# An encoder trunk in split fp32: h and the S forms at other SBUF addresses, S sums issued in the gate chunk

## The chip, the cores and the metric

The kernel runs on one core of a Trainium2 chip. The metric is the device time of one execution in microseconds (us).

## The reference

Two layers of a streaming encoder on 256 tokens with a model width of 2048, in float32. What matters here is the second half of each layer, the feed-forward part with an inner width of 5632:

```python
for l in range(DEPTH):
    ...                                   # attention, retention, w_out
    x = layer_norm(ALPHA * x + mix, ln1_g[l], ln1_b[l])
    f = (jax.nn.silu(x @ w_gate[l]) * (x @ w_up[l])) @ w_down[l]
    x = layer_norm(ALPHA * x + f, ln2_g[l], ln2_b[l])
return x
```

## The kernel before

**Split operands.** Each float32 operand is split into a high and a low part in a faster 4-byte format (ScalarE copies the high part, VectorE subtracts it for the low one, `split`, lines 249 to 251). A product is three matmuls: high by high, high weights' low part, low by high (lines 238 to 240, and 795 to 797). The activations are stationary, 128 by 128; the split weights are streamed, 512 columns. Weights come as units of 512 rows by 512 columns: a DMA on SP's queue brings a raw tile, the split fills one of three pairs of buffers `hi` and `lo` (lines 165 to 193), `W.get` hands the unit to the matmuls, and `W.done` prepares the unit that is three further on. One unit is 24 matmuls for both token halves.

**The feed-forward part.** The inner width is cut into 11 blocks of 512. Block 0 is the plain group (lines 769 to 783): a gate chunk of four units into the banks `gb`, SiLU on ScalarE, then the S forms, then an up chunk of four units into `ub`. Blocks 1 to 10 are Strassen groups (lines 785 to 861): for the first 1024 rows of `w_gate` and `w_up` the gate and the up product are joined by Strassen's scheme (the two token halves and the two weights form the 2 by 2 blocks), the other 1024 rows are multiplied plainly; together 15 products of 12 matmuls, in the banks sX, sQ, sW, sY, sZ and sR. Their stationary operands are slices of x (`xTh`, `xTl`) and the four S forms (`sfh`, `sfl`), sums of quarters of x that are computed once per layer: four subtractions on VectorE, 16 transposes on TensorE into banks `pts`, four splits (lines 744 to 755). A group's result is transposed into `hTh` and `hTl` by `flush`, eight transposes in banks `pth`, which the next group or the down-projection calls (lines 759 to 767). The blocks are taken in four parts of 3, 3, 2 and 3 blocks; behind each part comes its down-projection (lines 875 to 886) into banks `db`, with h stationary and the weights streamed, for four quarters of the output columns.

**Order.** The first three gate units are run for token half 0 and then for half 1 (`chunk_head`, lines 300 to 315), with the last pieces of the layer norm popped in between; these write the residual tile `res`, from which the S sums read. On each engine the instructions run in the order in which the program holds them.

**Addresses.** Tiles stand in SBUF in the order in which their pools first ask for them. In the program before, `hi` and `lo` stand at 192 modulo 256 bytes per partition, `xTh` and `xTl` at 128, `sfh` and `sfl` at 128, then a pad of 384 bytes (line 863), then `hTh` and `hTl` at 0, the vectors `v` at 0, and the raw tiles of the Strassen groups at 0.

Of the kernel before, what the change touches and what calls it, by code (L numbers as in the profile page):

```python
# [10 lines left out]
F32 = mybir.dt.float32  # L11
# [7 lines left out]
P = 128  # L19
# [92 lines left out]
def trunk(ctx: ExitStack, tc: tile.TileContext, x, pos, w, lnp, cols, eye, consts, out):  # L112
    nc = tc.nc
    V, A, PE, G = nc.vector, nc.scalar, nc.tensor, nc.gpsimd
# [8 lines left out]
    xTh = const.tile([P, KD, S], F32R, name="xTh")  # L123
    xTl = const.tile([P, KD, S], F32R, name="xTl")
# [7 lines left out]
    ident = const.tile([P, P], F32, name="ident")  # L132
    const.tile([P, 88], F32, name="pad0")

    def bank(tag_name):
        return psp.tile([P, 512], F32, tag="ps", name=tag_name)
# [96 lines left out]
    def mm_x(ps, ncol, tok, unit, xh, xl, k0, nk, first, last):  # L233
        wh, wl = unit
        for k in range(nk):
            sh = xh[:, k0 + k, tok * P:(tok + 1) * P]
            sl = xl[:, k0 + k, tok * P:(tok + 1) * P]
            PE.matmul(ps[:, :ncol], sh, wh[:, k, :ncol], start=first and k == 0, stop=False)  # L238
            PE.matmul(ps[:, :ncol], sh, wl[:, k, :ncol], start=False, stop=False)  # L239
            PE.matmul(ps[:, :ncol], sl, wh[:, k, :ncol], start=False, stop=last and k == nk - 1)  # L240
# [8 lines left out]
    def split(hi, lo, src):  # L249
        A.copy(hi, src)  # L250
        V.tensor_tensor(lo, src, hi.bitcast(F32), ALU.subtract)  # L251
# [36 lines left out]
    def pop(n=1):  # L288
        for _ in range(n):
            if pend:  # L290
                pend.pop(0)()

    def chunk_plain(banks, ncol, nu, xh, xl, k0, first=True, last=True):
        for u in range(nu):
            (unit,) = W.get()
            for tok in range(2):
                mm_x(banks[tok], ncol, tok, unit, xh, xl, k0 + 4 * u, 4, first and u == 0, last and u == nu - 1)
            W.done()

    def chunk_head(banks, ncol, nu, xh, xl):  # L300
        units = W.get(3)
        for u in range(3):
            mm_x(banks[0], ncol, 0, units[u], xh, xl, 4 * u, 4, u == 0, False)
            pop(1)
        pop(1)
        for u in range(3):
            mm_x(banks[1], ncol, 1, units[u], xh, xl, 4 * u, 4, u == 0, False)
            W.done()
            pop(1)
        pop(8)  # L310
        for u in range(3, nu):
            (unit,) = W.get()
            for tok in range(2):
                mm_x(banks[tok], ncol, tok, unit, xh, xl, 4 * u, 4, False, u == nu - 1)
            W.done()
# [55 lines left out]
    first = W.start()  # L371
# [45 lines left out]
    for l in range(DEPTH):  # L417
# [9 lines left out]

        cq = [bank(f"cq{t}") for t in range(2)]
        chunk_head(cq, 512, 4, xTh, xTl)
        if l == 0:  # L430
            rope_tables()
        ckv = [bank(f"ckv{t}") for t in range(2)]
        chunk_plain(ckv, 320, 4, xTh, xTl, 0)

        cqTh = att.tile([P, 4, S], F32R, tag="s1", name="cqTh")
# [117 lines left out]
        for t in range(2):  # L553
            pt = bank("pqr")
# [162 lines left out]
        mixh, mixl = Mix(mixAh, mixRh), Mix(mixAl, mixRl)  # L717
        wb = [bank(f"wo2{t}") for t in range(2)]
        chunk_plain(wb, 512, 4, mixh, mixl, 0)
        for t in range(2):  # L720
            resid(wb, 2, t, norm)
# [13 lines left out]
        ffp = ff_ctx.enter_context(tc.tile_pool(name=f"ff{l}", bufs=1))  # L735
        W.rpool = ff_ctx.enter_context(tc.tile_pool(name=f"rs{l}", bufs=3))
        normf = Norm(f"f{l}")
        sfh = ffp.tile([P, 4, 4, P], F32R, tag="sfh", name="sfh")
        sfl = ffp.tile([P, 4, 4, P], F32R, tag="sfl", name="sfl")

        def vt512(name):
            return ffp.tile([P, 512], F32, tag="v", bufs=8, name=name)

        def s_forms():
            x_ = lambda t, c: res[:, t, 512 * c:512 * (c + 1)]
            s1, s2, s3, s4 = (vt512(f"sf{i}") for i in range(4))
            V.tensor_tensor(s1, x_(1, 0), x_(1, 1), ALU.subtract)
            V.tensor_tensor(s2, x_(0, 0), s1, ALU.subtract)
            V.tensor_tensor(s3, x_(1, 0), x_(0, 0), ALU.subtract)
            V.tensor_tensor(s4, x_(0, 1), s2, ALU.subtract)  # L750
            for i, t in enumerate((s1, s2, s3, s4)):
                pt = bank("pts")
                for j in range(4):
                    PE.transpose(pt[:, j * P:(j + 1) * P], t[:, j * P:(j + 1) * P], ident)
                split(sfh[:, i, :, :], sfl[:, i, :, :], pt.rearrange("p (j t) -> p j t", j=4))

        hprev = []
# [10 lines left out]

        def plain_group(c, flush):
            gb = [bank(f"gb{t}") for t in range(2)]  # L770
            chunk_head(gb, 512, 4, xTh, xTl)
            sg = []
            for t in range(2):
                s_ = vt512("sg")
                A.activation(s_, gb[t], AF.Silu)
                sg.append(s_)
            flush()
            s_forms()
            ub = [bank(f"ub{t}") for t in range(2)]
            chunk_plain(ub, 512, 4, xTh, xTl, 0)  # L780
            for t in range(2):
                V.tensor_tensor(sg[t], sg[t], ub[t], ALU.mult)
                hprev.append((t, c, sg[t]))
# [76 lines left out]
            hprev.append((0, c, v2))  # L860
            hprev.append((1, c, v5))

        ffp.tile([P, 96], F32, tag="pad", name="pad1")
        for f0, f1 in FF_PARTS:
            nk = 4 * (f1 - f0)
            hTh = ffp.tile([P, 12, S], F32R, tag="hTh", name="hTh")
# [2 lines left out]
            for c in range(f0, f1):  # L869
                (strassen_group if c else plain_group)(c, flush)  # L870
            first, final = f0 == 0, f1 == NFF
            if final:
                g, b = ln_params(ffp, ("sfh", "sfl"), 2 + 2 * l)
            nu = f1 - f0
            for n in range(4):
# [11 lines left out]
                else:  # L887
                    last = l == DEPTH - 1
# [114 lines left out]
```

## Time and profile before

| | |
|---|---|
| median of 3 runs | 2230.58 us (2230.15 to 2232.27) |
| the profiled execution | 2230.7 us, its span 2228.9 us |
| TensorE busy | 2186.6 us of the span, 11084 matmuls |
| VectorE busy | 1590.7 us |
| ScalarE busy | 1025.6 us |
| mean granted TensorE clock | 0.995 |

TensorE's busy time counts overlapping matmuls once; a matmul's own duration is longer than the step from its start to the next one's start, as each overlaps the next. So steps are read from starts in the timeline.

### The profile page before, as it was taken

The numbers are of one execution on the slowest core, as the hardware profiler recorded it, in microseconds if no ns is written. First come the engines' busy times: TensorE is split into PE (matmuls) and PEld (weight loads), VectorE is DVE, ScalarE is ACT, GpSimd is POOL, SyncE is SP. The second block draws the span as 40 slices with busy tenths as digits, with TensorE's granted clock in tenths as the row PEclk, the third lists the DMA queues.
The fourth block names the chain that finished last, engine by engine and source line by source line (L and its number), as shares of the span: only waits on it lengthen the run. The fifth ranks groups of instructions, "written<-read, shape, count | busy, mean of one in ns | idle before, by whom it ended". The sixth has DMA issues, their size and how long they took to land.

```text
span 2228.9 us, 26855 instructions
## 1 busy us (share of the span) xinstructions
PE 2186.6 (98%) x11084; PEld 1839.3 (83%) x11084; DVE 1590.7 (71%) x1687; ACT 1025.6 (46%) x1089; POOL 35.5 (2%) x46
## 2 busy tenths in 40 slices
PE   6999999899999999999999999999999999999998
PEld 5988988788888888888889899877888888888886
DVE  7565676787588578788575656766966885877976
ACT  3554333455355345455344543334544553545552
POOL 0000000000000000000000000000000000000000
PEclk9999999999999999999999999999999999999999
DMA  7644554566567556476555444545665664666653
GB/s 254 212 151 154 182 197 168 207 208 226 170 225 250 199 195 233 162 245 200 198 185 187 147 171 170 208 170 189 225 231 180 234 236 166 203 245 208 208 208 114
DMA packets 63467, 441.22 MB, mean 198 GB/s; under 512 B 7408, under 2 KB 7664, under 8 KB 11504
## 3 DMA queue, kind: packets, MB, share of 16 engines
q1 hardware_dynamic: 60048, 418.46, 51.2%
q0 software_dynamic: 2880, 20.97, 5.2%
q8 instruction: 87, 1.43, 0.3%
q14 instruction: 36, 0.29, 0.0%
q10 hardware_dynamic: 416, 0.07, 0.0%
HBM read 437.38 MB, written 2.10 MB: 197 GB/s over the span
## 4 chain that ended last, share of the span: by engine, by line
PE 96%; DVE 2%; issue 1%; ACT 0%; DMA 0%; DVEq 0%; ACTq 0%
PE db L238 7%; PE db L240 7%; PE db L239 7%; PE sX L797 3%; PE sW L797 3%; PE sX L796 3%; PE sX L795 3%; PE sW L796 3%; PE sW L795 3%; PE prq L246 3%; PE prq L245 3%; PE prq L247 3%; PE wo L239 3%; PE wo L238 3%; PE sQ L797 2%; PE wo L240 2%
## 5 line engine op out<-in xcount | busy, mean ns | idle before, releaser
L251 DVE TENSOR_TENSOR lo<-raw,hi 128x1024 fp32r<-128x1024 f32 (+3 forms) x754 | 1033.5, 1406 | 438.3 <-ACT hi L250 435.8
L250 ACT CAST hi<-raw 128x1024 fp32r<-128x1024 f32 (+3 forms) x754 | 875.2, 1199 | 1004.4 <-PE db L240 306.9
L238 PE MATMUL db<-hi,hTh 128*128 128x512 f32 x704 | 279.6, 397 | 0.0
L239 PE MATMUL db<-lo,hTh 128*128 128x512 f32 x704 | 277.9, 395 | 0.0
L240 PE MATMUL db<-hi,hTl 128*128 128x512 f32 x704 | 275.3, 395 | 0.0
L238 PEld LDWEIGHTS db<-hi,hTh 128*128 128x128 f32 x704 | 132.0, 187 | 34.4 <-ACT hTh L250 3.6
L240 PEld LDWEIGHTS db<-hi,hTl 128*128 128x128 f32 x704 | 132.0, 187 | 32.5
L239 PEld LDWEIGHTS db<-lo,hTh 128*128 128x128 f32 x704 | 132.0, 188 | 31.2
L245 PE MATMUL prq<-xTh,hi 128*128 128x256 f32 x512 | 143.8, 281 | 0.0
L246 PE MATMUL prq<-xTl,hi 128*128 128x256 f32 x512 | 142.4, 278 | 0.0
L247 PE MATMUL prq<-xTh,lo 128*128 128x256 f32 x512 | 142.4, 278 | 0.0
L187 DVE TENSOR_TENSOR raw<-raw,raw 128x2048 f32<-128x2048 f32 x60 | 137.1, 2285 | 0.5
L797 PE MATMUL sX<-hi,xTl 128*128 128x512 f32 x320 | 126.3, 395 | 0.0
L795 PE MATMUL sX<-hi,xTh 128*128 128x512 f32 x320 | 125.6, 393 | 0.0
L796 PE MATMUL sX<-lo,xTh 128*128 128x512 f32 x320 | 125.6, 393 | 0.0
L245 PEld LDWEIGHTS prq<-xTh,hi 128*128 128x128 f32 x512 | 97.0, 189 | 0.1
L246 PEld LDWEIGHTS prq<-xTl,hi 128*128 128x128 f32 x512 | 96.2, 188 | 0.1
L247 PEld LDWEIGHTS prq<-xTh,lo 128*128 128x128 f32 x512 | 96.1, 188 | 0.0
L687 DVE SCALAR_TENSOR_TENSOR res<-res,db 128x512 f32<-128x512 f32 x64 | 43.8, 684 | 71.3 <-PE db L240 71.3
L797 PE MATMUL sQ<-hi,xTl 128*128 128x512 f32 x240 | 94.6, 394 | 0.0
L796 PE MATMUL sQ<-lo,xTh 128*128 128x512 f32 x240 | 94.2, 392 | 0.0
L795 PE MATMUL sQ<-hi,xTh 128*128 128x512 f32 x240 | 94.1, 392 | 0.0
(265 smaller groups left out, 3983.5 us busy)
## 6 DMA issues: line engine op xcount, KB each, us to landing
raw<-w SPq DMA_DIRECT2D x377, 1024.0 KB, 4.9
raw<-w POOLq DMA_DIRECT2D x20, 1024.0 KB, 8.7
raw<-w SPq DMA_DIRECT2D x8, 640.0 KB, 3.9
lng<-lnp SPq DMA_DIRECT2D x4, 1024.0 KB, 4.7
lnb<-lnp SPq DMA_DIRECT2D x4, 1024.0 KB, 5.8
res<-x SPq DMA_DIRECT2D x4, 512.0 KB, 6.4
out<-res SPq DMA_DIRECT2D x8, 256.0 KB, 2.6
cst<-consts SPq DMA_DIRECT2D x2, 976.5 KB, 8.2
```

What stands on the lines that cost most here:

```text
L187: V.tensor_tensor(r[into], r[into], r[frm], ALU.add)
L238: PE.matmul(ps[:, :ncol], sh, wh[:, k, :ncol], start=first and k == 0, stop=False)
L239: PE.matmul(ps[:, :ncol], sh, wl[:, k, :ncol], start=False, stop=False)
L240: PE.matmul(ps[:, :ncol], sl, wh[:, k, :ncol], start=False, stop=last and k == nk - 1)
L245: PE.matmul(ps_ap, wh[:, k, c0:c0 + P], xh[:, k, :], start=k == 0, stop=False)
L246: PE.matmul(ps_ap, wh[:, k, c0:c0 + P], xl[:, k, :], start=False, stop=False)
L247: PE.matmul(ps_ap, wl[:, k, c0:c0 + P], xh[:, k, :], start=False, stop=k == nk - 1)
L250: A.copy(hi, src)
L251: V.tensor_tensor(lo, src, hi.bitcast(F32), ALU.subtract)
L795: PE.matmul(ps, a, wh[:, k, :], start=first and k == 0, stop=False, skip_group_check=True)
L796: PE.matmul(ps, a, wl[:, k, :], start=False, stop=False, skip_group_check=True)
L797: PE.matmul(ps, b, wh[:, k, :], start=False, stop=k == 3, skip_group_check=True)
```

## The change

The pad of 384 bytes between the S forms and h goes. In its place stand a pad of 64 bytes ahead of the S forms and one of 192 bytes between them and h. The sums of the S forms (four subtractions) are issued inside the gate chunk, behind its third unit; the transposes and splits of the S forms are issued inside the up chunk: none ahead of its first unit, those of two forms ahead of the second, of one ahead of the third and of one ahead of the fourth. Nothing else is added or taken away.

```diff
-    def chunk_plain(banks, ncol, nu, xh, xl, k0, first=True, last=True):
+    def chunk_plain(banks, ncol, nu, xh, xl, k0, first=True, last=True, then=None):
         for u in range(nu):
+            if then is not None:
+                then(u)
             (unit,) = W.get()
...
-    def chunk_head(banks, ncol, nu, xh, xl):
+    def chunk_head(banks, ncol, nu, xh, xl, then=None):
...
         pop(8)
+        if then is not None:
+            then()
         for u in range(3, nu):
...
+        ffp.tile([P, 16], F32, tag="pad", name="pad1")
         sfh = ffp.tile([P, 4, 4, P], F32R, tag="sfh", name="sfh")
         sfl = ffp.tile([P, 4, 4, P], F32R, tag="sfl", name="sfl")
...
-        def s_forms():
+        sforms = []
+
+        def s_sums():
             x_ = lambda t, c: res[:, t, 512 * c:512 * (c + 1)]
-            s1, s2, s3, s4 = (vt512(f"sf{i}") for i in range(4))
+            sforms.extend(vt512(f"sf{i}") for i in range(4))
+            s1, s2, s3, s4 = sforms
             V.tensor_tensor(s1, x_(1, 0), x_(1, 1), ALU.subtract)
             V.tensor_tensor(s2, x_(0, 0), s1, ALU.subtract)
             V.tensor_tensor(s3, x_(1, 0), x_(0, 0), ALU.subtract)
             V.tensor_tensor(s4, x_(0, 1), s2, ALU.subtract)
-            for i, t in enumerate((s1, s2, s3, s4)):
+
+        def s_turn(u):
+            for i in ((), (0, 1), (2,), (3,))[u]:
                 pt = bank("pts")
                 for j in range(4):
-                    PE.transpose(pt[:, j * P:(j + 1) * P], t[:, j * P:(j + 1) * P], ident)
+                    PE.transpose(pt[:, j * P:(j + 1) * P], sforms[i][:, j * P:(j + 1) * P], ident)
                 split(sfh[:, i, :, :], sfl[:, i, :, :], pt.rearrange("p (j t) -> p j t", j=4))
...
-            chunk_head(gb, 512, 4, xTh, xTl)
+            chunk_head(gb, 512, 4, xTh, xTl, s_sums)
...
             flush()
-            s_forms()
             ub = [bank(f"ub{t}") for t in range(2)]
-            chunk_plain(ub, 512, 4, xTh, xTl, 0)
+            chunk_plain(ub, 512, 4, xTh, xTl, 0, then=s_turn)
...
-        ffp.tile([P, 96], F32, tag="pad", name="pad1")
+        ffp.tile([P, 48], F32, tag="pad2", name="pad2")
```

## Rows read from the trace of the kernel before

**Rows 1.** The page: shares of the chain that ended last, by engine.

```profile
PE 96%; DVE 2%; issue 1%; ACT 0%; DMA 0%; DVEq 0%; ACTq 0%
```

**Rows 2.** TensorE's waits: who waited for whom, us in total, times, longest.

```profile
PE pts L754 <- issue: 8.4, 2, 4.2
```

**Rows 3.** Windows: stretch, length, busy time of PE, PEld, DVE, ACT, POOL; PEclk; DMA.

```profile
418.90:426.60 7.70, 3.52 (x18) 3.28 (x17) 6.15 (x8) 4.13 (x6) 0.00 (x0) 0.78 0.73 272
423.20:426.60 3.40, 3.31 (x17) 3.28 (x17) 3.19 (x5) 1.65 (x3) 0.00 (x0) 0.50 0.86 304
427.00:1115.00 688.00, 688.00 (x3018) 558.75 (x3017) 514.64 (x418) 331.41 (x294) 9.83 (x11) 1.00 0.60 206
```

**Rows 4.** Timeline of PE (start, duration, instruction): a down-projection up to its flush.

```profile
532.84 0.39 PE L238 MATMUL db<-hi,hTh 128*128 128x512 f32 x1
...
544.04 1.03 PE L764 MATMUL pth<-ident,v 128*128 128x128 f32 x8
```

**Rows 5.** Timeline of PE: a Strassen part from its start to its first flush.

```profile
1894.93 0.40 PE L795 MATMUL sX<-hi,xTh 128*128 128x512 f32 x1
...
1944.39 1.03 PE L764 MATMUL pth<-ident,v 128*128 128x128 f32 x8
```

**Rows 6.** Timeline of PE: such a part in layer 0, up to its second flush.

```profile
601.02 0.40 PE L795 MATMUL sX<-hi,xTh 128*128 128x512 f32 x1
...
651.42 1.04 PE L764 MATMUL pth<-ident,v 128*128 128x128 f32 x8
652.21 0.48 PE L795 MATMUL sW<-hi,sfh 128*128 128x512 f32 x1
652.53 0.40 PE L796 MATMUL sW<-lo,sfh 128*128 128x512 f32 x1
...
693.52 1.04 PE L764 MATMUL pth<-ident,v 128*128 128x128 f32 x8
```

**Rows 7.** Timeline of PE: matmuls ahead of others whose stationary operand is a split weight.

```profile
63.23 0.31 PE L239 MATMUL ckv<-lo,xTh 128*128 128x320 f32 x1
63.38 0.31 PE L240 MATMUL ckv<-hi,xTl 128*128 128x320 f32 x1
63.52 0.29 PE L245 MATMUL pg<-xTh,hi 128*128 128x256 f32 x1
...
125.38 0.39 PE L240 MATMUL pr<-hi,cqTl 128*128 128x512 f32 x1
125.61 0.28 PE L245 MATMUL pkn<-ckT,hi 128*128 128x256 f32 x1
```

**Rows 8.** Timeline of DVE at the end of layer 0's gate chunk, idle time and releaser bracketed.

```profile
414.97 2.36 DVE L251 TENSOR_TENSOR lo<-raw,hi 128x1024 fp32r<-128x1024 f32 x2 [0.55 <-ACT hi L250]
420.23 2.36 DVE L251 TENSOR_TENSOR lo<-raw,hi 128x1024 fp32r<-128x1024 f32 x2 [2.90 <-ACT hi L250]
422.51 0.69 DVE L747 TENSOR_TENSOR sf<-res 128x512 f32<-128x512 f32 x1
...
425.04 0.69 DVE L251 TENSOR_TENSOR sfl<-pts,sfh 128x512 fp32r<-128x512 f32 x1
```

**Rows 9.** Timeline of PE between gate and up chunk, layer 0 and layer 1.

```profile
418.72 0.40 PE L240 MATMUL gb<-hi,xTl 128*128 128x512 f32 x1
423.29 3.55 PE L754 MATMUL pts<-ident,sf 128*128 128x128 f32 x16 [4.18 <-issue]
426.59 0.49 PE L238 MATMUL ub<-hi,xTh 128*128 128x512 f32 x1
...
1518.36 0.39 PE L240 MATMUL gb<-hi,xTl 128*128 128x512 f32 x1
...
1525.97 0.48 PE L238 MATMUL ub<-hi,xTh 128*128 128x512 f32 x1
```

**Rows 10.** Timeline of ACT at the end of layer 0's gate chunk.

```profile
419.15 1.99 ACT L250 CAST hi<-raw 128x1024 fp32r<-128x1024 f32 x2 [1.36 <-PE gb L240]
```

**Rows 11.** The weight loads of line 149 from 400 to 470 us: landing after issue.

```profile
DMA to landing us min/median/max: 4.7/5.8/9.2
```

## Prediction, made before the changed kernel was run

> **What bounds the kernel now.** I read the chain that ended last first: 96% of it is TensorE [rows 1]. So two things can shorten the run: TensorE's idle stretches, and the time from one matmul's start to the next one's. The waits come second: one of the largest waits of TensorE stands before the transposes of the S forms, 8.4 us in two times, put down to "issue" [rows 2]. The windows come third. Between the gate and the up chunk of layer 0's plain group TensorE does little, and the granted clock averages 0.78; in 427 to 1115 us it is busy throughout at full clock, and VectorE only 515 of 688 us [rows 3]. There nothing but the matmuls' own pitch counts, since no other engine holds TensorE up.
>
> The pitch is read from starts in the timeline, not from the 0.39 us of one matmul, which overlaps the next. I call "distance" the address of the split weights (the streamed operand, at 192 modulo 256 bytes in the program before) less that of the stationary operand. It is 64 for x and for the S forms (both at 128), and 192 for h (at 0). Every slice that a matmul takes of these tiles starts a multiple of 256 bytes into its tile, so all matmuls of a kind have one distance. The same 512-column matmul shows three cases:
> - h, distance 192: 48 matmuls from 532.84 to 544.04, 233.4 ns each [rows 4].
> - x, distance 64: the first 216 matmuls of a Strassen part (180 of one group, 36 of the next), 1894.93 to 1944.39, 229.0 ns each [rows 5].
> - x, again distance 64, such a part elsewhere: 216 from 601.02 to 651.42, 233.3 ns each, until eight transposes interrupt. The next 180, 652.21 to 693.52, take 229.0 again, with 0.09 us off for the first [rows 6].
>
> So the slow pitch comes with h, and sometimes outlives it: it looks like a rhythm between the stream and the next weight load that h's distance sets off and that lasts until the queue is disturbed. That is my reading; the rows show the three cases.
>
> **Part 1, the distance of h.** After the change the S forms stand 64 bytes further (at 192, distance 0), and h at 192 + 192 = 128 modulo 256, which is distance 64, x's. The queues get nothing. The down-projections run 11 blocks times 4 column quarters times 2 layers, 88 units of 24 matmuls, 2112 in all. At 233.4 less 229.0, 4.4 ns each, this is 9.3 us, all on the path, as TensorE is the chain there. Then the slow pitch that outlives h: four stretches of 216 matmuls (they start at 601, 796, 926 and 1700 us; the first stands here for all) take 50.40 us where the undisturbed one takes 49.46 [rows 5, 6], 0.94 us four times, 3.8 us. If h no longer sets the rhythm off, this goes too. Sum of part 1: 13.1 us; at the least 0 (rival 2).
>
> The tiles behind h (the values v, the raw weights of the Strassen groups) move by 128 bytes as well. VectorE reads them, with a quarter of its time free [rows 3], so I cost this at nothing; instructions 10% longer would make 566 of 688 us, still hidden.
>
> **Part 2, the S forms at distance 0.** They are stationary in 48 matmuls of each of 20 groups, 960 in all. The trace has no stretch at this distance, only single weight loads: where split weights are streamed and the next stationary operand is a split weight too. Such a matmul took 0.23 us at 125.38, the ordinary pitch, and a 320-column one 0.14 us at 63.38 where its neighbour took 0.15 [rows 7]. So one load shows no penalty. I take 228 ns, 1 ns less than now and nearest to these rows: 1.0 us gained. The bounds are the 10 ns by which that neighbour differs (9.6 us gained) and the slow 233.4 ns (4.2 us lost). A single load doesn't show which rhythm a run of twelve falls into; that is rival 1.
>
> **Part 3, the sums moved into the gate chunk.** Before, VectorE gets the four subtractions behind the last gate unit's weight split: the split starts at 420.23, the sums run from 422.51 to 425.04 [rows 8]. TensorE's last gate matmul starts at 418.72 and could be followed at 418.95; the transposes start at 423.29 and the up chunk at 426.59 [rows 9]. While they run the granted clock is 0.50, the lower level of 1.2 GHz [rows 3], after 4 us without work, and the 16 take 3.30 us, 0.21 each; in a flush eight take 0.79, 0.10 each [rows 6]. What goes: 426.59 - 418.95 = 7.64 us in layer 0, 1525.97 - 1518.59 = 7.38 in layer 1 [rows 9], and 0.09 each because the first matmul behind transposes takes 0.32 us to its successor instead of 0.23 [rows 6]: 15.2 us.
>
> What comes: the same 16 transposes between the units of the up chunk, in turns of eight, four and four. Eight take 0.79 us, and the matmul behind them 0.32 us instead of 0.23 [rows 6]: 0.88. Four are taken at half, 0.44. Together 1.76 per layer, 3.5 us, all on the path. The sums take 2.5 us of VectorE, which is free from 417.33 to 420.23 [rows 8]; the split behind them can't start sooner, as ScalarE's copy for it runs from 419.15 [rows 10]. Were they in its way for their whole length, it would end at 425.1 instead of 422.6, and its unit is read two units (11 us) behind the last gate matmul, at 430. So the sums cost nothing. The four copies and subtractions behind the transposes (0.6 and 0.7 us each) fall into the up chunk, where each engine splits one unit, 2 to 2.4 us, in the 5.5 us that TensorE takes for one. The S forms are first read in the third unit of the next group.
>
> Moved earlier with all this: the up chunk and all behind it, by 6 us. The weight loads are on SP's queue and wait for their buffers, and land 4.7 to 9.2 us after issue [rows 11]. The raw tile that is split first in the up chunk gets its buffer when the split before 414.97 ends [rows 8], so it is there by 424.2 at the latest, and its copy must wait for the unit that ends at 418.95 + 5.5 = 424.5. Thus no new wait; at worst one landing late, 1 to 2 us per layer. Net of part 3: 15.2 - 3.5 = 11.7 us, bounds 8 and 12.5.
>
> **Sum.** 11.7 + 9.3 + 3.8 + 1.0 = 25.8 us. The profiled execution took 2230.7 us with a span of 2228.9, 1.8 around it, and the median of the runs is 2230.6, so the profile stands for the median: 2230.6 - 25.8 = 2204.8, said as 2205. About 0.2% (4.5 us) is what a measurement of this kernel can tell from no change.
>
> **The rivals.** (1) The S forms at distance 0 fall into the slow rhythm. If it stays with the 960, the time is 2205 + 5.2 = 2210. If x keeps it as it did behind h, all 3600 Strassen matmuls are slow, 15.8 us less the 3.8 that are slow already, and the down-projections keep it until their flush (some 340 matmuls, 1.5 us): 2230.6 - 11.7 - 9.3 + 12.0 + 1.5 = 2223. For: how long it lasted in rows 6. Against: rows 7. Chance 0.16.
>
> (2) The distance has no say, and the slow pitch belongs to the stage (its order of banks and units). Then only part 3 is left, 2230.6 - 11.7 = 2219. For: x was seen at 233.3 too [rows 6]. Against: no stretch of h runs at 229. The Trainium skill, page "TensorE: Matmul & The Clock Gate", section "Step-by-step: what each phase is for", speaks for this rival: it says that TensorE reads the streamed operand and the next weights through two independent ports, so that loading takes nothing from the running matmul. By that rule the two rhythms of x at one clock in rows 5 and 6 would not be there, so the trace doesn't bear it out. Chance 0.14.
>
> (3) Slower than before. At distance 0 stream and weight load start in the same place of the 256 bytes at about the same time. If one has to wait for the other, the load no longer lies beside the matmul. The price of that is seen where a matmul follows transposes, 0.32 against 0.23 us [rows 6]: 960 times 0.087 is 83 us, 2289. It decides from 27 ns per matmul on (25.8 / 960), at a pitch of 255. Against: rows 7. Chance 0.03, and 0.03 for a lesser price of this kind that ends within 0.2% of before.
>
> **How the numbers follow.** The forecast itself has 0.64, between 2196 and 2214 by the bounds of parts 2 and 3. The range 2196 to 2220 takes in rival 2 and the lower part of rival 1. Faster: the forecast, rivals 1 and 2, 0.94; same 0.03; slower 0.03.
>
> **What would show it.** Right: 48 matmuls at the start of a down-projection in 11.0 us instead of 11.20; every Strassen stretch of 216 in about 49.4; no idle stretch of TensorE ahead of the up chunk, transposes of the S forms at 0.10 us each and no fall of the granted clock there. Wrong: db still at 233 (rival 2); sW, sY or sZ above 229 where an S form is stationary (rivals 1 and 3); or new waits of TensorE in the up chunk for a split, which would say that the gap had hidden the weights.

## The result and the profile after

The changed kernel takes 2206.18 us (median; 2205.77 to 2206.75) where the kernel before took 2231.43 in the same comparison: a ratio of 0.9885, 95% interval 0.9868 to 0.9902. The prediction was 2205, range 2196 to 2220. The profiled execution of the changed kernel took 2205.9 us with a span of 2204.1, 24.8 us less than the span of before.

The first view is TensorE's waits (who waited for whom, us in total, times, longest). The wait of [rows 2] is gone from the list. What leads it, the transposes of the layer norms, led it before as well, with 17.6 us; the longest of these waits, 11.5 us, is the start of the program.

```profile
PE ptx L282 <- DVE res L278: 17.2, 7, 11.5
```

The windows (stretch, length, busy time of PE, PEld, DVE, ACT, POOL; granted clock; DMA share; GB/s) answer [rows 3]: in the same stretch ahead of the up chunk TensorE is now busy throughout, and the granted clock is 1.00 instead of 0.78.

```profile
418.90:426.60 7.70, 7.70 (x39) 6.41 (x38) 3.34 (x3) 4.55 (x6) 0.00 (x0) 1.00 0.71 271
427.00:1100.00 673.00, 673.00 (x2992) 552.81 (x2992) 513.49 (x418) 329.79 (x294) 9.01 (x11) 1.00 0.62 211
```

The timeline of TensorE answers [rows 9]. The up chunk follows the gate chunk after one matmul's step (418.62 to 418.85). Eight transposes of S forms take 0.79 us, four take 0.35, and the matmul behind them is late by 0.09. Layer 0's plain group is 6.0 us shorter, layer 1's 5.8.

```profile
418.62 0.39 PE L240 MATMUL gb<-hi,xTl 128*128 128x512 f32 x1
418.85 0.39 PE L238 MATMUL ub<-hi,xTh 128*128 128x512 f32 x1
...
424.34 1.04 PE L764 MATMUL pts<-ident,sf 128*128 128x128 f32 x8
425.13 0.48 PE L238 MATMUL ub<-hi,xTh 128*128 128x512 f32 x1
425.45 0.40 PE L239 MATMUL ub<-lo,xTh 128*128 128x512 f32 x1
...
430.73 0.60 PE L764 MATMUL pts<-ident,sf 128*128 128x128 f32 x4
431.08 0.48 PE L238 MATMUL ub<-hi,xTh 128*128 128x512 f32 x1
```

On VectorE (timeline, answers [rows 8]) the sums end ahead of the split at 415.33, which is 0.36 us later than it was; the next one, at 420.13, is not late at all.

```profile
414.31 0.68 DVE L758 TENSOR_TENSOR sf<-res,sf 128x512 f32<-128x512 f32 x1
415.33 2.36 DVE L251 TENSOR_TENSOR lo<-raw,hi 128x1024 fp32r<-128x1024 f32 x2 [0.34 <-ACT hi L250]
420.13 2.36 DVE L251 TENSOR_TENSOR lo<-raw,hi 128x1024 fp32r<-128x1024 f32 x2 [2.44 <-ACT hi L250]
```

The pitch answers [rows 4] and [rows 6]. The first 48 matmuls of a down-projection take 11.00 us (229.2 ns each) instead of 11.20, and the first 216 of the Strassen part behind it 49.36 instead of 50.40. Twelve matmuls of sY with an S form take 2.72 us, 226.7 ns each.

```profile
526.63 0.39 PE L238 MATMUL db<-hi,hTh 128*128 128x512 f32 x1
...
537.63 1.04 PE L774 MATMUL pth<-ident,v 128*128 128x128 f32 x8
...
593.61 0.39 PE L804 MATMUL sX<-hi,xTh 128*128 128x512 f32 x1
...
642.97 1.04 PE L774 MATMUL pth<-ident,v 128*128 128x128 f32 x8
```

```profile
457.25 0.39 PE L804 MATMUL sY<-hi,sfh 128*128 128x512 f32 x1
...
459.97 0.39 PE L804 MATMUL sX<-hi,xTh 128*128 128x512 f32 x1
```

By starts of the stages in the two timelines, after less before, in us:

| stage | difference | predicted |
|---|---|---|
| plain groups, both layers | -11.8 | -11.7 |
| eight down-projections | -8.7 | -9.3 |
| Strassen parts: four slow stretches, 0.95 each | -3.8 | -3.8 |
| Strassen parts: the rest, S forms at distance 0 | -1.9 | -1.0 |
| attention of layer 0 and layer 1 | +0.1, +1.4 | 0 |
| sum | -24.7 | -25.8 |

### The profile page after: what moved, and what is told of

Same layout as the page of the kernel before. It is cut to its first block, busy times and chain, and to the rows that moved or that the text cites. A ratio compares the mean times of both kernels' runs of the same rounds, so it can differ in the third digit from the quotient of the medians.

```text
span 2204.1 us, 26848 instructions
## 1 busy us (share of the span) xinstructions
PE 2170.3 (98%) x11084; PEld 1838.2 (83%) x11084; DVE 1590.1 (72%) x1687; ACT 1024.4 (46%) x1089; POOL 35.5 (2%) x46
## 4 chain that ended last, share of the span: by engine, by line
PE 48%; DVE 2%; issue 0%; ACT 0%; DVEq 0%; ACTq 0%
PE db L238 4%; PE db L240 4%; PE db L239 4%; PE sX L805 2%; PE sX L804 2%; PE sW L805 2%; PE sW L804 2%; PE sX L806 2%; PE sW L806 2%; PE prq L246 1%; PE prq L247 1%; PE prq L245 1%; PE sQ L805 1%; PE sQ L804 1%; PE sQ L806 1%; PE wo L239 1%
```

## The experiments

The theory (A): the pitch of a matmul goes by the distance, and moving the sums takes out the idle stretch; the two are independent. The rivals: the moved sums changed the rhythm of what follows (B); S forms and h help only together (C). In the course of it a fourth question came up: whether the slow stretches of x belong to the kernel or to the execution (D). Where no ratio is given, the span and the pitches of one profile are compared. The kernel before alone took 2230.15 to 2234.34 us in its executions, so differences of a few us are read from stages and steps and not from one span.

**Addresses alone.** The kernel before with the two pads of the changed kernel.

```diff
+        ffp.tile([P, 16], F32, tag="pad", name="pad1")
         sfh = ffp.tile([P, 4, 4, P], F32R, tag="sfh", name="sfh")
...
-        ffp.tile([P, 96], F32, tag="pad", name="pad1")
+        ffp.tile([P, 48], F32, tag="pad2", name="pad2")
```

> The addresses of the changed kernel (S forms at distance 0, h at 64) with the sums left where they were. Theory A, the distance sets the pitch: the down-projections run at about 229.1 ns per matmul (11.0 us for the first 48), the four slow Strassen stretches of 216 fall from 50.40 to about 49.4 us, S forms near 227 ns, and the time falls by 13 to 14 us to about 2217. Rival B, the moved sums changed the rhythm of everything behind them: the down-projections stay at 233 ns or some stretches stay at 50.4 us, and the time falls by less than 6 us. The idle stretch of 7.4 to 7.7 us ahead of the up chunk stays in either case.

Measured: 2220.16 us against 2232.20, ratio 0.9944 (0.9929 to 0.9959). The down-projections lost 8.7 us and the Strassen parts 5.7, as in the changed kernel, and 48 matmuls take 11.00 us (timeline of TensorE):

```profile
424.49 3.65 PE L755 MATMUL pts<-ident,sf 128*128 128x128 f32 x16 [4.18 <-issue]
427.79 0.78 PE L238 MATMUL ub<-hi,xTh 128*128 128x512 f32 x1
428.37 0.63 PE L239 MATMUL ub<-lo,xTh 128*128 128x512 f32 x1
428.79 0.63 PE L240 MATMUL ub<-hi,xTl 128*128 128x512 f32 x1
...
534.61 0.39 PE L238 MATMUL db<-hi,hTh 128*128 128x512 f32 x1
...
545.61 1.04 PE L765 MATMUL pth<-ident,v 128*128 128x128 f32 x8
```

B falls. The time fell by 12.0 us instead of 13 to 14. In the profile the fall is 10.9 us, because the plain groups took 1.2 us more and the attention of each layer 1.1 us more than in the profile of before. The first of these stands in the rows: behind the idle stretch not only the 16 transposes but also the first matmuls of the up chunk run at the lower clock here (0.58 and 0.42 us to the next start; the granted clock is 0.50 from 424.49 to 429.43). So the idle stretch costs up to 1.3 us more in some executions than in the one of [rows 9].

**Sums alone.** The changed kernel with the pads of before (none ahead of the S forms, 384 bytes ahead of h).

```diff
-        ffp.tile([P, 16], F32, tag="pad", name="pad1")
...
-        ffp.tile([P, 48], F32, tag="pad2", name="pad2")
+        ffp.tile([P, 96], F32, tag="pad2", name="pad2")
```

> The sums and the transposes moved as in the changed kernel, with the addresses of the kernel before (S forms at 64, h at 192). Theory A: the plain groups lose 6.0 and 5.8 us, everything else stays within 1 us, the down-projections at 233.4 ns, slow Strassen stretches of 50.4 us still there behind some of them; about 11.8 us less, 2219 to 2220. Rival B: the down-projections become faster too, and the time falls by 20 us or more.

Measured: 2217.76 against 2232.20, ratio 0.9933 (0.9916 to 0.9950), 14.4 us. The plain groups lost 6.0 and 5.7 us; the down-projections stayed at 11.20 us for 48 matmuls. But no stretch behind a down-projection was slow, although h is at distance 192 (timeline of TensorE):

```profile
528.28 0.39 PE L238 MATMUL db<-hi,hTh 128*128 128x512 f32 x1
...
539.48 1.04 PE L773 MATMUL pth<-ident,v 128*128 128x128 f32 x8
...
596.48 0.40 PE L803 MATMUL sX<-hi,xTh 128*128 128x512 f32 x1
...
645.93 1.03 PE L773 MATMUL pth<-ident,v 128*128 128x128 f32 x8
```

216 matmuls in 49.45 us. The Strassen parts of this profile are 3.9 us shorter than before's, which takes the time beyond the expected 11.8 although the attention took 2.7 us more, and it contradicts what I had read into [rows 6], that h's place alone decides. Together the two halves give 26.5 us, the whole change 25.3.

**One tile each.** The S forms at distance 0 with h at 192, and h at 64 with the S forms at 64; sums in place.

```diff
+        ffp.tile([P, 16], F32, tag="pad", name="pad1")
         sfh = ffp.tile([P, 4, 4, P], F32R, tag="sfh", name="sfh")
...
-        ffp.tile([P, 96], F32, tag="pad", name="pad1")
+        ffp.tile([P, 16], F32, tag="pad2", name="pad2")
```

> Only the S forms moved to distance 0; h stays at 192, the sums stay in place. Theory A: matmuls with an S form as stationary operand take about 227 ns each instead of 229 (about 2 us in all), the down-projections stay at 233.4 ns, and the slow rhythm still outlives some of them (stretches of 50.4 us). If a run of S matmuls at distance 0 ends the slow rhythm, stretches behind it are not slow although no transposes came between. Rival C, the gain of the S forms is a by-product of h: they stay at 229 here.

The rows (timeline of TensorE) show 12 matmuls with an S form in 2.72 us and 48 with h in 11.20. So the S forms gain by themselves, and C falls for them.

```profile
464.93 0.39 PE L796 MATMUL sY<-hi,sfh 128*128 128x512 f32 x1
...
467.65 0.39 PE L796 MATMUL sX<-hi,xTh 128*128 128x512 f32 x1
...
534.34 0.40 PE L238 MATMUL db<-hi,hTh 128*128 128x512 f32 x1
...
545.54 1.03 PE L765 MATMUL pth<-ident,v 128*128 128x128 f32 x8
```

No stretch of 216 was slow as a whole (49.37 to 49.52 us), but three of the six began slow. In the one below the first 36 matmuls, with x, take 8.40 us, 233.3 ns each as in [rows 6]; the slow step ends in the first run of S forms, and x then goes on at 229, with no transposes in between. That is what the expectation asked: a run of S forms at distance 0 ends the slow rhythm.

```profile
602.52 0.40 PE L796 MATMUL sX<-hi,xTh 128*128 128x512 f32 x1
...
610.92 0.39 PE L796 MATMUL sW<-hi,sfh 128*128 128x512 f32 x1
...
652.04 1.04 PE L765 MATMUL pth<-ident,v 128*128 128x128 f32 x8
```

The span was 2228.4 us, hardly less than before's 2228.9: the Strassen parts lost 4.9 us, but the plain groups took 0.8 and 1.3 us more and the attention of the two layers 1.1 and 1.4. The gain of the S forms' own step, some 2 us, is too small to be seen in one span.

```diff
-        ffp.tile([P, 96], F32, tag="pad", name="pad1")
```

> Only h moved to distance 64 (the pad taken out); the S forms stay at 64, the sums in place. Theory A: down-projections at 229.1 ns, no stretch of 216 above 49.6 us, S matmuls at 229.0 ns; about 12.5 us less, span near 2216. Rival C, that h at 64 helps only beside S forms at 0: the down-projections or the stretches behind them stay at 233 ns in part, and less than 9 us are gained.

```profile
533.50 0.39 PE L238 MATMUL db<-hi,hTh 128*128 128x512 f32 x1
...
544.50 1.04 PE L764 MATMUL pth<-ident,v 128*128 128x128 f32 x8
```

48 matmuls in 11.00 us, all down-projections 8.6 us shorter, no slow stretch; span 2219.9 instead of the expected 2216, with plain groups 0.4 and 1.3 us longer and layer 1's attention 1.5 us longer than in the profile of before. Here h starts 256 bytes lower than in the changed kernel and has the same pitch, which fits a period of 256 bytes.

**The kernel before again, and the moved sums again.** Nothing is edited.

> The kernel before, unchanged, for a second profiled execution. Theory A, h at distance 192 leaves the queue in the slow rhythm by its place in the program: the same four Strassen stretches of 216 (behind the first, second and third down-projection of layer 0 and the first of layer 1) take 50.40 us again, the others 49.45. Theory D, which rhythm follows a down-projection is a matter of the execution: other stretches, or none, are slow, and the down-projections are at 233.4 ns as before. The span is then up to 4 us shorter.

> The kernel before once more, on the same chip and in the same call as the next run. Theory D, execution or chip decides whether the slow rhythm outlives a down-projection: any of the six Strassen parts behind a down-projection may be slow. If the chip decides, this run and the next one agree: both with slow stretches or both without. If the kernel decides, this one has three or four slow stretches as in its two profiles so far, and the next one none.

> The moved sums with the addresses of the kernel before, a second time. Its first profile had no slow stretch although h is at 192. If the kernel decides: none again, 83.3 and 125.4 us per Strassen part. If chip or execution decides: as in the run before it, some parts at 84.3 or 126.4 us.

In the second profile of before three of the six stretches were slow, and not the same ones. The part at 926 us, slow in the first, is undisturbed here, and the one at 1897 us, undisturbed in [rows 5], is slow (first profile below). In the third profile of before three were slow, among them the one at 927 us again. The moved sums had none in their first profile and three in their second, one of which is shown below (50.40 us). Both are timelines of TensorE.

```profile
926.60 0.40 PE L795 MATMUL sX<-hi,xTh 128*128 128x512 f32 x1
...
976.05 1.03 PE L764 MATMUL pth<-ident,v 128*128 128x128 f32 x8
...
1897.22 0.40 PE L795 MATMUL sX<-hi,xTh 128*128 128x512 f32 x1
...
1947.62 1.03 PE L764 MATMUL pth<-ident,v 128*128 128x128 f32 x8
```

```profile
788.75 0.40 PE L803 MATMUL sX<-hi,xTh 128*128 128x512 f32 x1
...
839.15 1.04 PE L773 MATMUL pth<-ident,v 128*128 128x128 f32 x8
```

So D holds as far as the kernel goes: one kernel has slow stretches in different places from one execution to the next, and within one execution some are slow and some not, so the chip alone doesn't fix it either. Over the five profiles with h at 192 and the S forms at 64 (three of before, two of the moved sums) 13 of 30 stretches were slow. Over six with h at 64 or 0 (the changed kernel, the addresses alone, h alone, and below the two of h at 0 and the one of x at 0) none of 36 even began slow.

The trace's starts, to the nanosecond, show one thing more. With h at 192 the last 24 steps of a down-projection are either even (231 to 234 ns) or uneven (229 to 236 ns), both with a mean of 233.0 to 233.4. In all six profiles with h at 192, the one with only the S forms moved included, a stretch of x began slow behind every one of the 16 even endings and behind none of the 20 uneven ones, where the first twelve matmuls average 230.0 ns at most and the rest 229. Why one pattern or the other comes is not shown.

**h at distance 0.** The changed kernel without its second pad; the two expectations below are both for this kernel.

```diff
-        ffp.tile([P, 48], F32, tag="pad2", name="pad2")
```

> The changed kernel with h at distance 0 too (the second pad taken out). Theory A with distance 0 as good for h as it is for the S forms: down-projections at 227 ns, some 4 us less than the changed kernel, span near 2200. Rival, that 227 ns hold only for runs of 12 between other stationary operands: the down-projections stay at 229 or go above.

> The changed kernel with h at distance 0, timed: down-projections at 227.0 ns, some 4.5 us less than the changed kernel's 2206, a ratio of about 0.986 to the kernel before. Rival, that the single look was a lucky execution: 2205 to 2207.

The first profile has a span of 2199.6 us. Timed, the kernel takes 2202.22 us against 2233.04, ratio 0.9863 (0.9846 to 0.9879): 4 us less than the changed kernel by the medians, while the two intervals overlap. The profile is clearer than the time. 48 matmuls take 10.88 us, 226.7 ns each, and the eight down-projections are 4.3 and 4.2 us shorter than the changed kernel's in its two profiles.

```profile
528.99 0.39 PE L238 MATMUL db<-hi,hTh 128*128 128x512 f32 x1
...
539.87 1.03 PE L774 MATMUL pth<-ident,v 128*128 128x128 f32 x8
```

**h at distance 128.**

```diff
-        ffp.tile([P, 48], F32, tag="pad2", name="pad2")
+        ffp.tile([P, 32], F32, tag="pad2", name="pad2")
```

> The changed kernel with h at distance 128 (second pad of 128 bytes). Theory A says only that the pitch goes by the distance: with 227 at 0, 229 at 64 and 233.4 at 192, a value between 229 and 236 ns, the same in all eight down-projections. Rival B, the pitch has nothing to do with the distance: 229 ns as in the changed kernel.

```profile
526.59 0.40 PE L238 MATMUL db<-hi,hTh 128*128 128x512 f32 x1
...
537.74 1.04 PE L774 MATMUL pth<-ident,v 128*128 128x128 f32 x8
```

11.15 us for 48, 232.3 ns. The gain of h at 64 is nearly gone, with the sums and the S forms as in the changed kernel: span 2210.4. This is theory A's expectation, against the rival that the distance has no say. Two of the six stretches behind a down-projection began slow here as well.

**x at distance 0, and at 96.** The kernel with h at 0, and 64 or 224 bytes of padding ahead of x; the last pad of that pool is shorter by as much, so the weights stay where they are.

```diff
     res = const.tile([P, 2, D], F32, name="res")
+    const.tile([P, 16], F32, name="padx")
...
-    const.tile([P, 88], F32, name="pad0")
+    const.tile([P, 72], F32, name="pad0")
```

> The changed kernel with x, h and the S forms all at distance 0 (64 bytes of padding ahead of x, the pad ahead of the weights shortened by as much). x is stationary in some 4800 matmuls of 512 columns: at 227 instead of 229 ns they gain 9 to 10 us, h another 4, so 2191 to 2194. Where x is streamed and the split weights are stationary (2570 matmuls of 256 columns, 116 ns now) the distance changes as well and the trace has no row for it: from -3 ns (8 us less) to +5 ns (13 us more).

Measured: 2204.9 us against 2231.91, ratio 0.9878 (0.9862 to 0.9895): no better than with x at 64, and a miss of the expected 2191 to 2194. The 512-column matmuls gained as expected, 216 in 48.97 us, 226.7 ns (first two rows). But the matmuls that stream x lost at least as much: 240 of them in layer 1's attention take 28.88 us, 120.3 ns each (last two rows). Against the two profiles of h at 0, the Strassen parts are 5.3 us shorter and the attention 6.4 and 8.6 us longer.

```profile
596.67 0.39 PE L805 MATMUL sX<-hi,xTh 128*128 128x512 f32 x1
...
645.64 1.03 PE L775 MATMUL pth<-ident,v 128*128 128x128 f32 x8
...
1167.10 0.36 PE L246 MATMUL pg<-xTh,hi 128*128 128x256 f32 x1
...
1195.98 0.29 PE L246 MATMUL pqn<-cqTh,hi 128*128 128x256 f32 x1
```

In the changed kernel the same 240 take 27.30 us in layer 0 and 28.35 in layer 1:

```profile
81.11 0.37 PE L245 MATMUL pg<-xTh,hi 128*128 128x256 f32 x1
...
108.41 0.28 PE L245 MATMUL pqn<-cqTh,hi 128*128 128x256 f32 x1
...
1167.01 0.36 PE L245 MATMUL pg<-xTh,hi 128*128 128x256 f32 x1
...
1195.36 0.28 PE L245 MATMUL pqn<-cqTh,hi 128*128 128x256 f32 x1
```

```diff
+    const.tile([P, 56], F32, name="padx")
...
-    const.tile([P, 88], F32, name="pad0")
+    const.tile([P, 32], F32, name="pad0")
```

> The kernel with h and S forms at distance 0, x at 96. If the pitch is a smooth function of the distance, 512-column matmuls with x lie between the 229 ns of 64 and the 232.7 of 128, so 1 to 3 ns more on some 4500 matmuls, 5 to 13 us; and the matmuls that stream x against split weights go the other way from what they did at 0 (120.5 ns there, 116 at 64), to 114 or 115, 3 to 5 us less. If only a few distances count (whether stream and load meet in one 64-byte piece), the pitch is as at 64 or as at 128 and nothing lies between.

A miss. 216 matmuls take 50.27 us, 232.7 ns, and that is a mean of two kinds: the first 36, all with x, take 8.40 us, 233.3 ns each, as much as h at 192, and neither the step at 64 nor the one at 128 nor one between them; the twelve S forms behind them take 2.77 us, 230.8 ns, though they stand at distance 0 as in the changed kernel, where they take 226.7. The streamed side became slower than at 64, too (117.6 and 119.0 ns by its starts, the faster of its two steps at 64 being 113.8). Span 2222.0.

```profile
598.11 0.39 PE L805 MATMUL sX<-hi,xTh 128*128 128x512 f32 x1
...
606.51 0.40 PE L805 MATMUL sW<-hi,sfh 128*128 128x512 f32 x1
...
609.28 0.39 PE L805 MATMUL sX<-hi,xTh 128*128 128x512 f32 x1
...
648.38 1.04 PE L775 MATMUL pth<-ident,v 128*128 128x128 f32 x8
```

So theory A holds only in part: the step goes with the place of the stationary operand in each case tried, but the S forms show that it depends on the matmuls around them, too.

## Why the prediction was right, point by point

**Part 3, the moved sums**, was right in size and place: 11.8 for 11.7 us. The transposes run at 0.10 us each, the clock doesn't fall, no wait replaced the old one, and the weights of the up chunk were there. The kernel with the sums alone shows the same 11.7, with nothing else moved. What the sum did not have is that the idle stretch is dearer in other executions, when the lower clock lasts into the up chunk.

**Part 1, h**, was right: 8.7 for 9.3 us. The term was slightly too large because 48 matmuls show 4.2 ns of gain each, not 4.4 (11.20 us over 48 is 233.3 ns, not the 233.4 of the sum). h at 64 alone gives it, and h at 0, 64, 128 and 192 gives 226.7, 229.2, 232.3 and 233.3 ns for the same matmuls in the same order. This decides against rival 2, that the stage makes the pitch. The values v and the raw tiles moved along with h each time and were not moved by themselves; that x keeps its 229 ns in the Strassen parts wherever they stand speaks against them.

**Part 1, the slow rhythm that outlives h**, has the right cause, h's place, and the wrong certainty. The four stretches and their 3.8 us were real in the profiled pair, and no kernel with h at 64 shows them. But I took one execution for the kernel: the three profiles of before have 4, 3 and 3 slow stretches of six, and the moved sums, with h at the same place, none and 3; over all five that is 2.6 of six, 2.5 us. The step that fails is "four stretches ... 3.8 us" as a property of the program. "Until the queue is disturbed" fails as well: a run of S forms at distance 0 ends the slow step without any transposes.

**Part 2, the S forms**, went the way I took and further: 226.7 to 227 ns instead of 228, 1.9 for 1.0 us. Rivals 1 and 3 needed a pitch of 233 or 255 ns there; a run of twelve loads at distance 0 shows no penalty, like the single ones of [rows 7].

**What was not in the sum** is +1.4 us in layer 1's attention. It is no effect of the change: 1.05 us of it are the 240 matmuls that stream x and take 27.30 or 28.35 us, and most of the rest lies in matmuls beside them. The profile of before had the short time in both layers, its second profile the long one, and the kernels above mix them. So matmuls with x streamed have two rhythms as well, and the first profile of before was a lucky one in that place. It was also a somewhat unlucky one behind the down-projections, with four slow stretches where the other two had three. That 2205 met 2206 within about 1 us is in part luck: the terms miss by 0.1, 0.6, 0.9 and 1.5 us, and not all the same way.

By the Trainium skill, page "TensorE: Matmul & The Clock Gate", section "Step-by-step: what each phase is for", the streamed operand and the next weights have independent read ports; if nothing else set the pitch, only part 3 would have been left, an estimate of 2219 us. The trace doesn't agree with this estimate: at full clock and with no other engine waited for, moving one operand by 64 or 128 bytes changes the pitch between 226.7 and 233.3 ns.

Two things stay open. In all kernels the split weights stand at 192, so distance and the stationary tile's own address were not told apart for 512 columns; moving the weights was not tried. That both at 192 is the best case with x stationary and the worst of the three tried with x streamed speaks against a rule by the distance alone. And why one rhythm or the other sets in is not shown; the rows show only what the slow one lasted to: transposes in [rows 6], a run of S forms at distance 0 in the kernel with these alone.

## What to carry to other kernels

Where a kernel's chain is all TensorE, read the step between starts by operand pair: two tiles that differ only in their address modulo 256 bytes differed by up to 3% here, and a pad is the whole edit. Check each role of a tile: the address that is best for x as stationary operand cost at least as much again where x is streamed. A term read from one execution should be looked up in a second one before it stands as a property of the program.

## What the runs showed of the hardware

- The step of a 512-column matmul against the distance of split weights and stationary operand, all with the weights at 192: 0, 226.7 ns (S forms, h and x alike); 64, 229; 96, 233.3 (x); 128, 232.3 (h); 192, 233.3 (h). It is not smooth: 96 is no better than 128. It is not the operand's own distance alone: S forms at distance 0 take 226.7 ns among x at 64 or 0 and 230.8 among x at 96.
- At one and the same distance a run can have two steps, 229.0 and 233.3 ns with x stationary at 64 [rows 5, 6], 113.8 and 118.1 ns (27.30 and 28.35 us for 240) with x streamed. Which of them is taken varies from execution to execution, and behind h at 192 with the pattern in which the down-projection ends: even steps, slow; uneven ones, fast, in 36 of 36. A run of twelve matmuls with S forms at distance 0 ended the slow one in five of five (three with h at 192, two at 128).
- In the 4 us without work ahead of the S transposes the granted clock fell to 1.2 GHz (0.50 in [rows 3]). It was back when the 16 transposes ended in [rows 9], but only at 429.43, in the fourth matmul of the up chunk, in the kernel with the addresses alone. There the idle stretch was dearer by 0.8 us.
